# A hybrid decoder layer with sparse experts: scores moved into the first u piece, rows requested earlier, the sort's steps and transfers a piece apart, more v rows beside u blocks

## The chip, the cores and the metric

The kernel runs on one core of one Trainium2 chip. The metric is the device time of one execution in microseconds. The median of three runs of the kernel before is 3421.0 us (3416.03, 3421.0 and 3427.66).

## What is computed

One layer for 512 prompt tokens and 64 sample tokens (576 in all), width 2048: adaptive normalisation, one input projection, a gated linear recurrence and a short convolution, an output projection, and then PEER, a layer of 16384 single-neuron experts with product keys. The change touches PEER alone:

```python
def peer(h, w_q, sub_keys, expert_u, expert_v):
    ...
        q = (xb @ w_q).reshape(PEER_BLOCK, PEER_HEADS, 2, HALF_DIM)
        sc = jnp.einsum('thpk,pnk->thpn', q, sub_keys).astype(jnp.float32)
        v1, i1 = lax.top_k(sc[:, :, 0], PEER_TOPK)
        v2, i2 = lax.top_k(sc[:, :, 1], PEER_TOPK)
        cand = (v1[..., :, None] + v2[..., None, :]).reshape(...)
        cidx = (i1[..., :, None] * N_KEYS + i2[..., None, :]).reshape(...)
        top, pos = lax.top_k(cand, PEER_TOPK)
        eidx = jnp.take_along_axis(cidx, pos, axis=-1)
        g = jax.nn.softmax(top, axis=-1).astype(xb.dtype)
        act = jax.nn.gelu(jnp.einsum('td,thkd->thk', xb, expert_u[eidx])) * g
        return jnp.einsum('thk,thkd->td', act, expert_v[eidx])
```

Each token has 8 heads and 16 picks a head, 128 picks; a pick is a row of `expert_u` (2048 numbers) multiplied with the token, and a row of `expert_v` added to its result with a weight.

## The kernel before

**Dense blocks and gathered rows.** The first key of a pick names one of 128 blocks of 128 experts. For the prompt tokens the 84 blocks that are picked most (`L`) are computed densely on TensorE for all 512 tokens, with the gates of experts that were not picked at zero. What is left over of the prompt's picks, and all picks of the sample tokens, are gathered: an indirect transfer issued by POOL (`take`, L1131) brings one row for each of 128 partitions, a tile of 128 x 2048, and VectorE forms its product with the token (a u row, L1159, `u`) or adds it to a sum (a v row, L1185, `accB`). Tokens are put in groups for this (`GT`; group 0 is the samples, the others are prompt tokens sorted by the number of their left-over picks), so that a group of many picks gets many rows. There are 216 uses of u rows, in groups that end at uses 64, 99, 143, 177, 205 and 216, and 211 of v rows. Row buffers: 4 during the u phase (`RB`), 6 after it (`RV`). A use at a group's end reads the next group's token vectors first (`h2r`, L1140).

**Phases.** Until 1240.7 us of the span come the normalisation, the projections, the recurrence, the queries and their top 16. The u phase, 1240.7 to 2349.5, is 168 pieces, half a block each: 24 matmuls (L1270, `u_half`) on a 512 KB piece of the u table (`raw<-ut`, loaded by SP three pieces ahead) that ACT and POOL split two pieces ahead into a high and a low part (`xhi` L842, `xlo` L843). Each finished block goes through a Gelu and out to memory (`act`, `actd`). The v phase, 2349.5 to 3269, is 84 steps of four columns, 12 matmuls each (L1290, `v_column`), whose sums VectorE adds up (`acc`, L1312). The samples' sums and the final normalisation follow.

**What runs beside the u pieces.** The loop over the pieces `n` issues, ahead of the matmuls of each piece, some of the other work. An allowance `spare` grows by `PIECE` (5.5) a piece, beginning at `-BEHIND`; while it is positive, the next step of a generator is issued, and the cost that the step yields is taken off (also 2.4 for a used row and 2.2 for a pair of gate blocks). A `None` from the generator ends the piece's steps.

- `choice()` (`steps1`) comes first. It finishes the last head: scores of the sample tokens ("S") and of the four prompt tiles (`score`, matmuls and copies), `choose`, `resolve`, `softmax`. Then `count()` marks the picks outside the dense blocks (`flags`, L1000 to L1004) and writes the picked values to memory with eight transfers on POOL's queue (`pickd`, L1010 and L1011); twelve transposes (`ptr`, L1414) turn the picks for the gates (`it`, L1416); `sort()` ranks the tokens: `srt` (L1021), four steps z of comparing and one-hot building on VectorE (L1032, L1034, L1041) with five small matmuls each (ten passes in the trace; `tokp`, L1043), and a last sum (`overp`, L1058). When it ends, at piece `R1`, the gates begin.
- The gates, from `R1` on: 128 blocks of one-hot products, put together in pairs on VectorE (`g_pair`, L1449, `op` and `wr`), scaled on ACT (`g_scale`, L1457), multiplied on TensorE (`g_mm`, L1463, into `gbank`) and copied out by ACT (`g_out`, L1470). `g_one` issues a block's matmuls, once ahead of a piece and once in its middle (`mid`).
- `all_slots()` (`steps2`), also from `R1` on: for each group of tokens the rows it needs are picked out (`slot_rows`, `pick_keys`, L1066 to L1110). It ends at piece `R2`. `ready[0]` is the last use whose list is made.
- Rows: until `R2`, `gather_to` uses up `due_g`, which grows by the first number of `RATE` a piece before `R1` and by the second after it, and is held by `ready[0]`; a row is requested up to `RB - 1` uses ahead. After `R2` the remaining u rows and the first `EARLY_V` v rows are spread evenly over the pieces that are left.

In the built program of before, the lists of group 0 are ready at piece 6 and the first row is requested and used at piece 8; `R1` is 46 and `R2` is 147; 222 rows are used in the u phase.

Of the kernel before, what the change touches and what calls it, by code (L numbers as in the profile page):

```python
# [5 lines left out]
F32 = mybir.dt.float32  # L6
# [32 lines left out]
QT = NA // 128  # L39
SORTED = ((0, 64, 34), (64, 128, 43), (192, 128, 33), (320, 128, 27), (448, 64, 10))  # L40
RB = 4
# [1 line left out]
ENDS = 5  # L43
LATE = 1
PIECE = 5.5
BEHIND = 18.0
RATE = (0.75, 1.55)
HEADS_COUNTED = 4
FULL_ROWS = 1.25
LAG = 2  # L50
PAIRS = 6
EARLY_V = 6
HB = 4
SB = 10
TK = 16
# [21 lines left out]
def build(ctx, tc, A, O, dbg=None):  # L77
# [912 lines left out]
    def count():  # L990

        m = nd["m"] = rt.tile([128, 3, QT], F32, name="nd_m")
        fc = rq.tile([128, 2, NA], F32, name="flags", tag="oh", bufs=2)
        fl, code = fc[:, 0, :], fc[:, 1, :]
        i1, i2 = pbank("g", "i1", 2), iselP[:, 1, :]
        S.activation(i1, iselP[:, 0, :], AF.Copy)
        yield None
        V.tensor_scalar(fl, i1, perm[:, L:L + 1], None, op0=ALU.is_equal)
        for x in range(L + 1, 128):
            V.scalar_tensor_tensor(fl, i1, perm[:, x:x + 1], fl, op0=ALU.is_equal, op1=ALU.add)  # L1000
            if x % 8 == 7:
                yield 5.0
        V.scalar_tensor_tensor(code, i1, 128.0, i2, op0=ALU.mult, op1=ALU.add)
        V.scalar_tensor_tensor(code, code, 1.0, fl, op0=ALU.add, op1=ALU.mult)  # L1004
        V.tensor_reduce(m[:, 0, :], fl.rearrange("p (z k) -> p z k", k=NPK), axis=AX.X, op=ALU.add)
        for z in range(QT):
            V.tensor_scalar(m[:, 1, z:z + 1], rowi, float(128 * z), None, op0=ALU.add)
        V.scalar_tensor_tensor(m[:, 2, :], m[:, 0, :], float(NA), m[:, 1, :], op0=ALU.mult, op1=ALU.add)
        for z in range(QT):
            G.dma_start(pickd[z * 128:(z + 1) * 128, 0:NPK], code[:, z * NPK:(z + 1) * NPK])  # L1010
            G.dma_start(pickd[z * 128:(z + 1) * 128, NPK:], topv[z].rearrange("p h k -> p (h k)"))  # L1011
        yield 5.0
        for _ in range(2):
            yield None

    def sort():

        m = nd["m"]
        pr = pbank("g", "srt", 2)
        for z in range(QT):  # L1020
            PE.matmul(pr[:, z * 128:(z + 1) * 128], m[:, 2, z:z + 1].to_broadcast([128, 128]), ident, start=True, stop=True)  # L1021
        allk = pools["rsort"].tile([128, NA], F32, name="allk")
        S.activation(allk, pr, AF.Copy)
        io = pools["rsort"].tile([128, NA], F32, name="io512")
        for z in range(QT):
            V.tensor_scalar(io[:, z * 128:(z + 1) * 128], iota, float(128 * z), None, op0=ALU.add)
        yield None
        pt = pbank("g", "tokp", 2)
        rk = pools["rsort"].tile([128, QT], F32, name="rk")
        for z in range(QT):  # L1030
            oh = pools["rsort"].tile([128, NA], F32, name=f"ohs{z}", tag="ohs", bufs=2)
            V.scalar_tensor_tensor(oh, allk, m[:, 2, z:z + 1], ones[:, 0:1].to_broadcast([128, NA]),  # L1032
                                   op0=ALU.is_gt, op1=ALU.mult, accum_out=rk[:, z:z + 1])
            V.tensor_scalar(oh, io, rk[:, z:z + 1], None, op0=ALU.is_equal)  # L1034
            for i, (p0, n, c) in enumerate(GT):
                if p0 is None:
                    continue
                lhs = oh[:, p0:p0 + n]
                if n < 128:
                    lhs = pools["rsort"].tile([128, 128], F32, name=f"ohd{i}_{z}", tag="ohd", bufs=2)  # L1040
                    V.tensor_copy(lhs.rearrange("p (r t) -> p r t", t=n),  # L1041
                                  oh[:, None, p0:p0 + n].to_broadcast([128, 2, n]))
                PE.matmul(pt[:, 2 * i:2 * i + 2], lhs, m[:, 0:2, z], start=z == 0 and i == 1,  # L1043
                          stop=z == QT - 1 and i == len(GT) - 1)
            yield 4.0
        srt = pools["rsort"].tile([128, len(GT), 2], F32, name="sorted")
        V.memset(srt[:, 0, 0:1], 0.0)
        V.tensor_scalar(srt[:, 0, 1:2], rowi, float(NA), float(T - 1), op0=ALU.add, op1=ALU.min)
        V.tensor_copy(srt[:, 1:, :], pt[:, 2:2 * len(GT)].rearrange("p (i a) -> p i a", a=2))
        V.tensor_copy(tok, srt[:, :, 1])  # L1050

        for i, (p0, n, c) in enumerate(GT):
            cap = c * 128 // n if i else NPK
            V.tensor_scalar(srt[:, i, 0:1], srt[:, i, 0:1], -float(cap), 0.0, op0=ALU.add, op1=ALU.max)
        over = pools["rsort"].tile([128, 1], F32, name="over")
        V.tensor_reduce(over, srt[:, :, 0], axis=AX.X, op=ALU.add)
        pf = pbank("g", "overp", 2)
        PE.matmul(pf[:, 0:1], ones, over, start=True, stop=True)  # L1058
        V.tensor_copy(flag, pf[0:1, 0:1])
        yield 1.0  # L1060

# [152 lines left out]
    def gather_to(n, lim=1 << 30):  # L1214

        n = min(int(n), lim)
        while gu[0] < min(n, len(uses)):
# [4 lines left out]
            gu[0] += 1  # L1222
            flush(gu[0])

    def load_group(sg, j):

        if j == 0:
            acts[sg] = ep.tile([128, SG, NA], F32, name=f"actr{sg}", tag="actr", bufs=1)
            nc.scalar.dma_start(acts[sg], actd[SG * sg:SG * sg + SG].rearrange("i p t -> p i t"))
        else:  # L1230
            gsb[sg] = ep.tile([128, NCH, SG * TC], F32, name=f"gsb{sg}", tag="gsb", bufs=1)
            nc.scalar.dma_start(gsb[sg], gd[:, :, sg * SG:(sg + 1) * SG, :].rearrange("c p i t -> p c (i t)"))
# [20 lines left out]
    g2 = mods[5]  # L1253
    fin = {}

    def mid(n):
        if R1 is not None and gk:
            g_one(n)

# [111 lines left out]
    def choice():  # L1371

        side, h = {}, HD - 1
        order = ["S"] + late
        side["S"] = score(h, "S")
        picked = iter(())
        yield None
        for a, z in enumerate(order):
            if a + 1 < len(order):
                side[order[a + 1]] = score(h, order[a + 1])  # L1380
            choose(h, side[z], z)
            yield 6.0
            if z == "S":
                for _ in resolve("S", 0):
                    yield 9.0
                yield 5.0
                picked = pick_samples()
            yield next(picked, 0.0)
            yield next(picked, 0.0)
# [18 lines left out]
        for j in range(3):  # L1408
            it.append(itp.tile([128, NA], F32, name=f"it{j}"))
        for i in range(QT):  # L1410
            pt = pbank("g", f"ptr{i}", 2)
            t = topv[i].rearrange("p h k -> p (h k)")
            for j, src in enumerate((isel[i][:, 0, :], isel[i][:, 1, :], t)):
# [67 lines left out]

    E0 = NU2 - 14
    steps1, steps2 = choice(), all_slots()
    spare, due_g = -BEHIND, 0.0
    R1 = R2 = None
    gm = [0, 0, 0, 0]
# [12 lines left out]
    for n in range(NU2):  # L1499
# [3 lines left out]
        if n == 1:  # L1503
            sample_rows()
        ahead(n + 3, n + 2)
        spare += PIECE
        if R1 is not None:
            put(2)
            g_one(n)
# [9 lines left out]
            gm[3] = gm[0]  # L1519

        if R2 is None:
            due_g += RATE[R1 is not None] if ready[0] else 0
            g0 = gu[0]
            gather_to(due_g, ready[0])
            due_g = min(due_g, gu[0] + 1.0)
# [253 lines left out]
```

## Time and profile before

| | |
|---|---|
| median of three runs | 3421.0 us |
| profiled execution | 3418.08 us |
| its span | 3416.3 us |
| granted TensorE clock, mean | 0.961 |
| TensorE busy | 3196.4 us (94%) |
| VectorE, POOL, ACT busy | 2164.3, 1752.5, 1083.4 us |
| DMA | 868.17 MB, 254 GB/s in the mean |

Times in the profile are microseconds from the start of the span. TensorE is PE, VectorE DVE, ScalarE ACT, GpSimd POOL, SyncE SP. Each row of the groups has line, engine, operation, output and inputs, count, then busy time and the mean of one in ns, then the idle time ahead of it and what ended that. A row of waits names the waiting instruction's line, the one that ended the wait, the total, how many times, and the longest. A row of windows has the stretch and its length, the busy time and count of each engine asked for, the granted clock, the DMA engines' share and GB/s. Rows of the chain and of the timeline start with the time and the duration.

### The profile page before, as it was taken

What the parts mean: (1) busy time and instruction counts of PE and PEld (TensorE: products, weight loads), DVE (VectorE), ACT (ScalarE), POOL (GpSimd) and SP (SyncE); (2) the same over time, 40 slices, a digit from 0 to 9 for tenths busy, and PEclk for the clock granted to TensorE, in tenths of its full rate; (3) what the DMA queues carried; (4) which work ended last, traced back from release to release, by engine and by line L of the source; (5) the groups of instructions that cost most, each with busy time, mean ns of one, the idle gap of its engine ahead of it and who ended that gap; (6) DMA issues with size and microseconds to landing.
All of it is one profiled execution on the core that took longest, in us unless ns stands there. A gap on an engine that the chain in (4) does not pass through costs nothing.

```text
span 3416.3 us, 47510 instructions
## 1 busy us (share of the span) xinstructions
PE 3196.4 (94%) x17641; PEld 2710.3 (79%) x17641; DVE 2164.3 (63%) x3246; ACT 1083.4 (32%) x1665; POOL 1752.5 (51%) x993
## 2 busy tenths in 40 slices
PE   5899999989979999989999999998999999999887
PEld 2698788989969988878888888876888777777776
DVE  5355522143346887968786787766677777787735
ACT  3234311132232232315555555522322222222122
POOL 4233233344333336646555566566767766676742
PEclk8899999999989999989999999998999999999988
DMA  9644466634442137759986979899999988898954
GB/s 337 231 139 139 160 208 205 216 114 128 130 138 71 66 102 255 263 186 366 340 302 259 376 284 370 317 365 334 369 386 368 368 297 330 301 393 297 337 170 148
DMA packets 304029, 868.17 MB, mean 254 GB/s; under 512 B 36618, under 2 KB 80522, under 8 KB 255658
## 3 DMA queue, kind: packets, MB, share of 16 engines
q1 hardware_dynamic: 165152, 390.35, 33.5%
q0 software_dynamic: 62896, 386.64, 29.0%
q10 hardware_dynamic: 75744, 88.09, 7.3%
q8 instruction: 139, 2.28, 0.3%
q14 instruction: 98, 0.80, 0.1%
HBM read 864.69 MB, written 68.90 MB: 273 GB/s over the span
## 4 chain that ended last, share of the span: by engine, by line
PE 39%; DMA 9%; DVE 8%; issue 5%; POOL 3%; ACT 0%; SPq 0%; POOLq 0%; ACTq 0%; DVEq 0%
PE pu L1270 19%; PE pv L1290 15%; PE gbank L1463 3%; DMA v<-v,rows 3%; DMA gsb<-gd 2%; DMA actr<-actd 2%; DVE u L1159 2%; DVE accB L1185 2%; DMA raw<-v 1%; POOL xlo L843 1%; DVE flags L1000 1%; POOL u L1131 1%; DMA h2r<-h2d,tok 0%; DVE oh L728 0%; PE pv L1294 0%
## 5 line engine op out<-in xcount | busy, mean ns | idle before, releaser
L843 POOL TENSOR_TENSOR xlo<-raw,xhi 128x1024 fp32r<-128x1024 f32 x336 | 818.4, 2447 | 643.9 <-ACT xhi L842 637.0
L842 ACT ACTIVATE xhi<-raw 128x1024 fp32r<-128x1024 f32 x336 | 354.1, 1059 | 922.9 <-PE pv L1290 466.1
L1159 DVE SCALAR_TENSOR_TENSOR u<-u,hT 128x2048 f32<-128x2048 f32 x211 | 479.5, 2284 | 242.5 <-DMA u<-u,rows 242.0
L1185 DVE SCALAR_TENSOR_TENSOR accB<-v,dots,accB 128x2048 f32<-128x2048 f32 x205 | 482.4, 2353 | 156.3 <-DMA v<-v,rows 154.5
L1290 PE MATMUL pv<-ahi,xhi 128*128 128x512 f32 x1344 | 540.9, 402 | 31.3 <-DVE acc L1312 24.2
L1290 PE MATMUL pv<-ahi,xlo 128*128 128x512 f32 x1344 | 538.3, 401 | 17.0 <-POOL xlo L843 16.9
L1270 PE MATMUL pu<-hhi,xhi 128*128 128x512 f32 x1344 | 543.4, 404 | 4.3 <-ACT xhi L842 4.3
L1270 PE MATMUL pu<-hhi,xlo 128*128 128x512 f32 x1344 | 529.8, 394 | 7.5 <-POOL xlo L843 7.5
L1290 PE MATMUL pv<-alo,xhi 128*128 128x512 f32 x1344 | 534.8, 398 | 0.0
L1270 PE MATMUL pu<-hlo,xhi 128*128 128x512 f32 x1344 | 531.4, 395 | 0.0
L1290 PEld LDWEIGHTS pv<-ahi,xhi 128*128 128x128 f32 x1344 | 257.8, 192 | 93.1 <-issue 16.7
L1290 PEld LDWEIGHTS pv<-ahi,xlo 128*128 128x128 f32 x1344 | 257.3, 191 | 82.8 <-POOL xlo L843 22.8
L1270 PEld LDWEIGHTS pu<-hhi,xlo 128*128 128x128 f32 x1344 | 254.8, 190 | 67.8 <-POOL xlo L843 10.4
L1290 PEld LDWEIGHTS pv<-alo,xhi 128*128 128x128 f32 x1344 | 258.0, 192 | 58.6
L1270 PEld LDWEIGHTS pu<-hhi,xhi 128*128 128x128 f32 x1344 | 255.6, 190 | 57.5 <-ACT xhi L842 5.6
L1270 PEld LDWEIGHTS pu<-hlo,xhi 128*128 128x128 f32 x1344 | 255.5, 190 | 50.1
L1131 POOL DMA_INDIRECT v<-v,rows x211 | 249.2, 1181 | 58.3 <-issue 32.5
L1131 POOL DMA_INDIRECT u<-u,rows x211 | 221.3, 1049 | 72.1 <-DVE u L1159 32.3
L1457 ACT ACTIVATE op<-op,it 128x128 f32<-128x128 f32 x512 | 154.3, 389 | 0.0
L185 PE MATMUL ada<-wa,cpad 128*32 128x512 f32 x768 | 112.5, 691 | 42.9 <-DMA wa<-w_ada 42.9
L1463 PEld LDWEIGHTS gbank<-wr,op 128*128 128x128 f32 x1024 | 135.5, 193 | 18.7 <-ACT op L1457 8.0
L122 POOL TENSOR_TENSOR wlo_q<-raw_q,whi_q 128x1024 fp32r<-128x1024 f32 x28 | 67.4, 2407 | 146.1 <-ACT whi_q L120 146.1
(477 smaller groups left out, 5574.9 us busy)
## 6 DMA issues: line engine op xcount, KB each, us to landing
wa<-w_ada SPq DMA_DIRECT2D x96, 1024.0 KB, 6.4
raw<-ut SPq DMA_DIRECT2D x168, 512.0 KB, 5.8
raw<-v SPq DMA_DIRECT2D x336, 256.0 KB, 8.0
actd<-act ACTq DMA_DIRECT2D x84, 256.0 KB, 7.1
gd<-stg ACTq DMA_DIRECT2D x64, 336.0 KB, 8.8
actr<-actd ACTq DMA_DIRECT2D x21, 1024.0 KB, 21.3
gsb<-gd ACTq DMA_DIRECT2D x21, 1024.0 KB, 26.2
raw_o<-w_out SPq DMA_DIRECT2D x32, 512.0 KB, 3.8
```

What stands on the lines that cost most here:

```text
L122: lo_engine(share).tensor_sub(lo, raw, r32(hi))
L185: PE.matmul(acc[32 * g:32 * g + 32, :], cpad[:, 4 * kq + g, :], w[:, g, :], start=kq == 0, stop=kq == 3)
L842: S.activation(hi, raw, AF.Copy)
L843: G.tensor_sub(lo, raw, r32(hi))
L1000: V.scalar_tensor_tensor(fl, i1, perm[:, x:x + 1], fl, op0=ALU.is_equal, op1=ALU.add)
L1131: G.indirect_dma_start(out=out, out_offset=None, in_=src, in_offset=bass.IndirectOffsetOnAxis(ap=idx, axis=0), bounds_check=NE * 128 - 1, ...
L1159: V.scalar_tensor_tensor(r, r, 1.0, st["h"], op0=ALU.mult, op1=ALU.mult, accum_out=dots[i][:, j:j + 1])
L1185: V.scalar_tensor_tensor(st["a"], r, dots[i][:, j:j + 1], st["a"], op0=ALU.mult, op1=ALU.add)
L1270: PE.matmul(pu, st[:, kk, :], movA[mv](k), start=k == 0 and a == 0, stop=k == KD - 1 and a == 2)
L1290: PE.matmul(pv, st, mv, start=first and j == 0 and a == 0, stop=last and not end and j == SG - 1 and a == 2)
L1457: S.activation(ops[:, j0 + j, :], ops[:, j0 + j, :], AF.Copy, scale=it[2][:, b * 4 + j:b * 4 + j + 1])
L1463: PE.matmul(pg[:, j * L:(j + 1) * L], ops[:, j0 + j, :], wr[:, j0 + j, :], start=True, stop=True)
```

## The change

It has five parts.

1. The first step of `choice()` is issued in the middle of piece 0, and the scores of the samples and of the first prompt tile are both in it; before, it was issued where `spare` first allowed it, with the samples' scores alone. `BEHIND` falls from 18 to 7, so `spare` becomes positive earlier.
2. The piece after the lists of group 0 are ready is noted in `since`; two pieces before the first use three rows are requested together (`fetch_to`). Before, the first row was requested at the piece of its use.
3. `count()` ends its costed step, and one piece, ahead of the eight transfers on POOL's queue; the transposes are halved over two pieces; in `sort()` the matmuls of each z are issued behind the next z's VectorE work, with four buffers where there were two, and the end of the sort and its last sum stand a piece apart.
4. `RATE` rises from (0.75, 1.55) to (1.0, 1.7), and `spare` grows by 6.3 (`PIECE_G`) a piece from `R1` on, where it grew by 5.5.
5. `EARLY_V` rises from 6 to 20: 14 v rows more, all of group 0, are used in the u phase and as many fewer in the v phase.

In the built program after the change the group 0 lists are ready at piece 4, three rows are requested at piece 6 and the first is used at piece 8; `R1` is 53 and `R2` is 122; 236 rows are used in the u phase.

```diff
-BEHIND = 18.0
-RATE = (0.75, 1.55)
+BEHIND = 7.0
+RATE = (1.0, 1.7)
+PIECE_G = 6.3
...
-EARLY_V = 6
+EARLY_V = 20
...
+        yield 5.0
+        yield None
         for z in range(QT):
             G.dma_start(pickd[z * 128:(z + 1) * 128, 0:NPK], code[:, z * NPK:(z + 1) * NPK])
             G.dma_start(pickd[z * 128:(z + 1) * 128, NPK:], topv[z].rearrange("p h k -> p (h k)"))
-        yield 5.0
         for _ in range(2):
             yield None
...
+        hot = []
+
+        def count_up():
+            for out, lhs, rhs, first, last in hot:
+                PE.matmul(out, lhs, rhs, start=first, stop=last)
+            hot.clear()
+
         for z in range(QT):
...
+            todo_ = []
             for i, (p0, n, c) in enumerate(GT):
...
-                    lhs = pools["rsort"].tile([128, 128], F32, name=f"ohd{i}_{z}", tag="ohd", bufs=2)
+                    lhs = pools["rsort"].tile([128, 128], F32, name=f"ohd{i}_{z}", tag="ohd", bufs=4)
...
-                PE.matmul(pt[:, 2 * i:2 * i + 2], lhs, m[:, 0:2, z], start=z == 0 and i == 1,
-                          stop=z == QT - 1 and i == len(GT) - 1)
+                todo_.append((pt[:, 2 * i:2 * i + 2], lhs, m[:, 0:2, z], z == 0 and i == 1,
+                              z == QT - 1 and i == len(GT) - 1))
+            count_up()
+            hot.extend(todo_)
             yield 4.0
+        yield None
+        count_up()
...
         pf = pbank("g", "overp", 2)
+        yield None
         PE.matmul(pf[:, 0:1], ones, over, start=True, stop=True)
+        yield None
         V.tensor_copy(flag, pf[0:1, 0:1])
         yield 1.0
...
+    def fetch_to(n):
+        while gf[0] < n and row_free():
+            fetches[gf[0]]()
+            gf[0] += 1
...
+    mids = {}
+
     def mid(n):
+        for f in mids.pop(n, ()):
+            f()
         if R1 is not None and gk:
             g_one(n)
...
         order = ["S"] + late
-        side["S"] = score(h, "S")
+        for z in order[:2]:
+            side[z] = score(h, z)
         picked = iter(())
         yield None
         for a, z in enumerate(order):
-            if a + 1 < len(order):
+            if a and a + 1 < len(order):
                 side[order[a + 1]] = score(h, order[a + 1])
...
         for i in range(QT):
+            if i == 2:
+                yield None
             pt = pbank("g", f"ptr{i}", 2)
...
     steps1, steps2 = choice(), all_slots()
+    mids[0] = [lambda: next(steps1)]
+    since = None
...
-        spare += PIECE
+        spare += PIECE if R1 is None else PIECE_G
...
-            due_g += RATE[R1 is not None] if ready[0] else 0
+            if since is None and ready[0]:
+                since = n
+            if since is not None and n == since + 1:
+                fetch_to(RB - 1)
+            due_g += RATE[R1 is not None] if since is not None and n > since + 2 else 0
```

## The prediction

> **What bounds the kernel now.** I read the head of the page first, then cut the time from 1249.7 us on into stretches by counting TensorE's matmuls at the two lines that set the pace, and last read what PE waited for in the stretches that came out too long.
>
> ```profile
> span 3416.3 us, 47510 instructions
> PE 3196.4 (94%) x17641; PEld 2710.3 (79%) x17641; DVE 2164.3 (63%) x3246; ACT 1083.4 (32%) x1665; POOL 1752.5 (51%) x993
> ```
>
> PE is busy for 94% of the span. No matmul of the dense work is added or removed, so the change can only win or lose what PE loses. The stretches of the u phase (matmuls of L1270 only, 24 to a piece; columns: length, PE busy and matmuls, weight loads, granted clock, DMA share, GB/s) and of the v phase (L1290, 12 to a column):
>
> ```profile
> 1249.70:1472.80 223.10, 221.74 (x961) 179.95 (x962) 1.00 0.69 241
> 1472.80:1524.10 51.30, 26.40 (x98) 20.22 (x96) 0.77 0.42 154
> 1546.20:1692.50 146.30, 128.15 (x529) 96.98 (x528) 1.00 0.94 355
> 1692.50:1712.80 20.30, 13.97 (x49) 10.43 (x49) 0.83 0.95 367
> 1858.30:1877.80 19.50, 12.96 (x48) 9.66 (x48) 0.91 0.99 382
> 1877.80:2235.90 358.10, 314.62 (x1297) 238.65 (x1298) 1.00 0.89 339
> 2263.40:2349.50 86.10, 72.16 (x289) 55.54 (x288) 0.94 0.88 321
> ...
> 2349.50:2396.60 47.10, 38.95 (x144) 29.66 (x145) 0.86 0.97 356
> 2396.60:2663.20 266.60, 266.00 (x1154) 216.24 (x1153) 1.00 0.98 368
> 2663.20:3269.10 605.90, 568.50 (x2390) 456.53 (x2389) 0.97 0.89 325
> ```
>
> Undisturbed rates come from the rows with clock 1.00: 223.1 us for 961/24 = 40 pieces, 5.58 us each; 146.3 us for 22 pieces with gate blocks between them, 6.65 us; 266.6 us for 96 v columns, 2.78 us. The other rows are longer than their count at these rates. Four pieces (41 to 44) took 51.3 us, 29 over 4 x 5.58. Pieces 71/72 and 95/96 took 20.3 and 19.5, over 13.3: 7.0 and 6.2. The last 12 u pieces took 86.1, over 67: 19. The first 12 columns took 47.1, over 33.3: 14. The last v row took 605.9 us for 199 columns, over 553: 53. That is 128 us in six places; the waits of PE there say what was late.
>
> ```profile
> PE ptr L1414 <- ACT it L1416: 6.4, 1, 6.4
> PE tokp L1043 <- issue: 5.0, 1, 5.0
> PE ptr L1414 <- DVE flags L1003: 2.3, 1, 2.3
> ...
> PE gbank L1463 <- ACT op L1457: 3.3, 1, 3.3
> ...
> PE gbank L1463 <- ACT op L1457: 3.8, 1, 3.8
> ...
> PE pu L1270 <- POOL xlo L843: 7.5, 6, 1.7
> PE pv L1290 <- ACT acc L1310: 4.9, 1, 4.9
> ...
> PE pv L1290 <- DVE acc L1312: 24.2, 9, 5.7
> PE pv L1290 <- POOL xlo L843: 13.6, 6, 7.1
> ```
>
> In order: the sort (1472 to 1530), the two changes of row group (1686 to 1715, 1850 to 1880), the end of the u phase with the first columns (2235 to 2397), and the v phase after it. The idle time is smaller than the excess because PE is slow after a stall, seen at the first group change:
>
> ```profile
> 1703.94 0.63 PE L1270 MATMUL pu<-hlo,xhi 128*128 128x512 f32 x1
> ...
> 1711.07 0.39 PE L1270 MATMUL pu<-hhi,xlo 128*128 128x512 f32 x1
> ```
>
> The first kind takes 0.63 us, the second 0.39; some ten of the slow ones make 2.4 us, and I use 2.5 per stall. [...]
>
> **Part by part.** How pieces move I read from the order of the two built programs on each engine; only the prices are from the trace. Pieces are numbered from 0, and a step that the schedule puts "at" a piece is issued ahead of its matmuls.
>
> *The sort (before: pieces 41 to 44).* Its own matmuls stay, and its waits move:
>
> ```profile
> 1488.09 1.54 PE ptr L1414 x6
> 1496.73 0.89 PE srt L1021 x8
> 1508.07 8.66 PE tokp L1043 x40
> ...
> 1504.41 0.75 DVE L1032 SCALAR_TENSOR_TENSOR ohs<-allk,nd_m,ones 128x512 f32<-128x512 f32 x1
> ...
> 1508.02 0.74 DVE L1032 SCALAR_TENSOR_TENSOR ohs<-allk,nd_m,ones 128x512 f32<-128x512 f32 x1
> ```
>
> The flags end at piece 41, the picked values are written at 44, and the transposes come at 46 and 47. So the 6.4 and 2.3 us of waits go. The eight writes of picked values move with them on POOL's queue:
>
> ```profile
> L1010 POOL DMA_DIRECT2D pickd<-flags x4 | 2.2, 557 | 14.6 <-DVE flags L1004 14.6
> L1011 POOL DMA_DIRECT2D pickd<-topv x4 | 2.2, 548 | 0.0
> ```
>
> There they waited 14.6 us at the queue's head for the flags, with a row and a conversion behind them; issued three pieces after the flags they wait for nothing and hold the queue for 4.4 us, which the two-piece lead of the conversions hides (without it, 4.4 on PE). But by then the allowance has grown to 20, so all four 4.0 steps of the rank counting still run at one piece, 49: the spreading is only partly done. The matmuls of each z stand behind the next z's VectorE work, those of z 0 to 2 still ahead of piece 49, the last ones at 50. PE at 49 then waits for a row product and the first counts, about 7 us where it was 5.0 (the second product in line, 2.3, and one z, from 1504.41 to 1508.02 at most 3.6, mostly 1.9). Sum: transposes 2.4, srt 0.9, wait 7, z 0 to 2 6.5, slow restart 2.5, last z 2.2: 21.5 against 29, so -8. Bounds: -20 if the counts are ready in time, +2 if each z waits for its own row.
>
> *Slots of group 1.* In the old order its five steps fall at pieces 47 to 61; in the new one all five (5, 4, 4, 4, 4) fall at piece 54, and the first pair of gate blocks stands behind them on VectorE at 55.
>
> ```profile
> 1538.71 0.22 DVE L1066 TENSOR_SCALAR sl<-R 128x128 uint32<-128x128 uint32 x1
> ...
> 1544.24 0.28 DVE L1099 MATCH_REPLACE8 kk<-sl,kk 128x128 f32<-128x128 f32 x1
> 1544.44 1.21 DVE L1449 TENSOR_TENSOR op<-kb,it 128x1024 f32<-128x1024 f32 x1
> ...
> 1701.24 2.40 ACT L1457 ACTIVATE op<-op,it 128x128 f32<-128x128 f32 x8
> ```
>
> The first two steps took 5.7 us (1538.71 to 1544.44): 2.2 for the keys and 3.55 for each step of six picks, so 16.4 for all. With the row's product VectorE is about 5 us into piece 54 when it begins; then come the slots, the pair (2.1) and half the scaling (1.2): 24.7 us after piece 54 begins. The first gate matmuls are due before piece 57, 3 x 5.5 = 16.5 us after it. PE waits 8.2 and restarts slowly, 2.5: +10.7. Bounds: 0 if the slots are done under earlier row waits, +16.
>
> *Group changes.* Before, rows 64 and 99 on (groups 1 and 2) each waited for the next group's hidden rows, read only once the list was ready: 7.0 and 6.2. In the new order list 1 is ready at piece 64, where use 64 is reached, so the first stall stays. List 2 is ready when its use is far off (143 ready at piece 80, at 91 uses), so the second goes: -6.2. Bounds -13 and 0.
>
> *Scores inside piece 0 and earlier rows.* VectorE begins the last head three pieces earlier. PE has no wait in pieces 1 to 40 (221.74 of 223.10 us busy), so nothing is won there; what hides it is the same row of PE work. The rows of uses 0 to 2 are requested two pieces ahead, and VectorE's first wait for a row shrinks. Value 0, bounds -3 and +3 (scores' matmuls standing in front of piece 0's second half).
>
> *Rate and early v rows.* The new rates bring 64 uses by piece 64, where the old order had them at 68; the u phase ends with 236 rows used, where it was 222. Its last 16 pieces take 1.6 a piece and took 1.9, but the last 20 are full v rows.
>
> ```profile
> L1159 DVE SCALAR_TENSOR_TENSOR u<-u,hT 128x2048 f32<-128x2048 f32 x211 | 479.5, 2284 | 242.5 <-DMA u<-u,rows 242.0
> L1185 DVE SCALAR_TENSOR_TENSOR accB<-v,dots,accB 128x2048 f32<-128x2048 f32 x205 | 482.4, 2353 | 156.3 <-DMA v<-v,rows 154.5
> L1131 POOL DMA_INDIRECT v<-v,rows x211 | 249.2, 1181 | 58.3 <-issue 32.5
> ...
> q0 software_dynamic: 8249, 59.95, 56.6%
> ```
>
> At the u phase's end PE waits for xlo and xhi, made from raw blocks that came late. A row is 1 MB, a raw piece 0.5, the activations 0.13: 1.6 rows make about 2.2 MB in 5.58 us, 396 GB/s; 1.9 rows with fewer of them full made 2.15, 385. So little is relieved: -5 of the 19 (bounds +10 and -15). The v phase loses 14 rows of 205: 33 us of VectorE (14 x 2.35), 17 of POOL, and 14.7 MB of transfers, which at the 368 GB/s of its second row are 40 us of DMA time out of 919, or 4%. Its stalls come to 14 + 53 = 67 us, and most are accumulations queued behind products that wait for rows. I take a fifth of them, -14; bounds 0 (the columns run at full speed at share 0.98, so the stalls are not saturation alone) and -40 (all of that transfer time was late).
>
> [...]
>
> **Sum:** -8 + 10.7 - 6.2 + 0 - 5 - 14 = -22.5. The profiled execution took 3418.1 us, 1.8 beyond its span, and gives 3395.6. The median of the runs is 2.9 above the profiled time; between the two bases I say 3397.
>
> **Rivals.** *VectorE falls behind from piece 54 on (slower).* Between pieces 54 and 122 the new order puts 116 products, 45 pairs of gate blocks and the slots of four groups on VectorE: 116 x 2.21 (2.28 less the overlap with the next) + 45 x 2.07 + 65 (the slots of all groups, 103 planned units at the 5.7/9 of above) is 414 us, in 68 x 6.65 = 452 us of PE. That leaves 38 for waits. In 22 such pieces before, it waited for rows
>
> ```profile
> DVE u L1159 <- DMA u<-u,rows: 22.7, 17, 4.8
> ```
>
> so 68 pieces would ask for 70. If the rows stay as late as that, 32 us come out of PE through the gate blocks, with two more slow restarts: 3397 + 32 + 5 = 3434. Against it: a VectorE that is late finds its rows landed, and waits shrink. It decides once waits per piece stay above 38/68 = 0.56 us while PE waits for gate matmuls.
>
> [...]
>
> *The v phase's stalls go by most of their size*, -40, with the sort's waits hidden: 3397 - 26 - 6 = 3365. For it speaks that all three resources of a row are relieved at once; against it, that 14 rows in 205 leave 93% of the load.
>
> *The change doesn't spread the sort as it says*: this is in the forecast already, at pieces 49 and 54. If instead both lumps cost nothing, 3397 - 10.7 - 9.5 = 3377.
>
> **How the numbers follow.** Two measurements of this kernel tell apart about 0.3%, 10 us: faster is below 3411, slower above 3431. The forecast (3380 to 3410) has 0.45, the deep gain and the lumps at nothing 0.13, the lost v gain 0.16 (mostly within 0.3%), VectorE behind 0.26. Faster 0.45 + 0.13 = 0.58; slower 0.21 of VectorE's 0.26 and 0.03 of the lost gain's 0.16 = 0.24; the rest, 0.18, is the same. The range runs from 3366 to 3440: about a tenth lies below, in the deep gain, and a tenth above, beyond VectorE's price. The forecast's own range is 3378 to 3412.
>
> **What would show it.** Right: no PE wait at the transposes; one stall of 5 to 9 us at piece 49 and one at 57, each with slow matmuls behind it; one group stall instead of two; the last 12 u pieces in 80 us or so; v columns from 2663 on with less than 53 us over 2.78 each. Wrong: VectorE without row waits and PE waiting on ACT's scaling through pieces 57 to 122 (VectorE behind); unchanged DVE waits in the v phase (v rows free of charge); conversions late from piece 122 on (transfers).

## The result and the profile after

The changed kernel takes 3399.01 us (median of 8 runs, 3393.41 to 3406.68) beside 3423.73 us for the kernel before (8 runs, 3416.03 to 3433.95): ratio 0.9934, 95% interval 0.9917 to 0.9952. (The ratios here are those on record with their intervals; the two medians alone give 0.9928.) A second measurement gave 0.9940 (0.9918 to 0.9961). So the kernel is faster, by 0.6 to 0.7%, which is small but clear of the noise. The forecast was 3397, faster.

The head of the page of the changed kernel:

```profile
span 3396.0 us, 47497 instructions
PE 3183.6 (94%) x17641; PEld 2699.9 (80%) x17641; DVE 2155.1 (63%) x3246; ACT 1084.6 (32%) x1665; POOL 1739.4 (51%) x993
```

The span is 20.3 us shorter, 3.4 of it ahead of the u phase, which starts at 1237.3 instead of 1240.7. The change touches nothing there, and the start lay between 1237.3 and 1243.5 in the profiles of this study: 16.9 us remain. The windows of the u matmuls (now L1295) show where:

```profile
1237.30:1469.30 232.00, 226.79 (x984) 184.44 (x985) 1.00 0.78 269
1469.30:1510.10 40.80, 39.34 (x169) 31.23 (x168) 1.00 0.82 279
1510.10:1538.30 28.20, 13.23 (x48) 10.25 (x49) 0.76 0.55 218
1571.70:1597.00 25.30, 13.00 (x50) 9.71 (x48) 0.80 0.72 258
...
1651.00:1671.90 20.90, 13.88 (x49) 10.41 (x49) 0.84 0.92 350
1792.70:1809.60 16.90, 11.86 (x48) 8.77 (x49) 1.00 0.92 335
2057.70:2073.80 16.10, 11.83 (x49) 8.81 (x49) 1.00 1.01 411
...
2228.60:2345.90 117.30, 103.08 (x432) 82.56 (x432) 0.94 0.92 349
```

and those of the v matmuls (now L1315):

```profile
2345.90:2390.40 44.50, 38.40 (x145) 29.64 (x146) 0.84 0.94 346
2390.40:2664.30 273.90, 269.43 (x1153) 217.94 (x1152) 0.99 0.96 354
2664.30:3250.20 585.90, 559.95 (x2389) 451.35 (x2388) 0.98 0.86 315
```

Pieces 0 to 40 take 232.0, as before (9.0 + 223.1). Pieces 41 to 47 run freely (40.8 for seven, 1.7 over their rate), where four pieces lost 29 before. The sort's stall is now at 48/49 (28.2 for two, 17.0 over), a new one is at 56/57 (25.3, 14.1 over, some 2 of it gate blocks), the first group change is at 66/67 (7.6 over 13.3), the second at 86/87 (3.6 over), and a small one has come at 125/126 (2.8 over). So pieces 0 to 150 lost 2.6 us net. From 150 to the first column it is 117.3 where it was 120.1, the first 12 columns take 44.5 (47.1 before), the next 96 are slower at 273.9 (266.6), and the 199 after them take 585.9 (605.9). That is 307 of the 336 columns; the other 29 come after 3250 (after 3269 before), among the last work on the samples. PE's waits between 1490 and 2236, from there to 2397, and from there to 3269:

```profile
PE gbank L1491 <- ACT op L1485: 13.3, 2, 9.3
PE tokp L1036 <- issue: 7.7, 1, 7.7
PE gbank L1491 <- ACT stg L1498: 4.7, 2, 2.7
...
PE pv L1315 <- ACT xhi L843: 9.2, 1, 9.2
PE pv L1315 <- POOL xlo L844: 6.1, 3, 3.2
...
PE pv L1315 <- POOL xlo L844: 17.1, 5, 7.8
PE pv L1315 <- DVE acc L1337: 13.3, 9, 3.0
```

The two waits at the transposes are gone. PE waits 7.7 us for the counting (7 in the forecast) and 9.3 for the first gate operands (8.2 in the forecast), and the accumulations that held the v columns for 24.2 us now hold them for 13.3. VectorE's timeline at piece 48 tells why PE waits for the counting: two more products and the index rows (`io`) stand ahead of the first z.

```profile
1514.74 2.29 DVE L1175 SCALAR_TENSOR_TENSOR u<-u,hT 128x2048 f32<-128x2048 f32 x1 [1.84 <-DMA u<-u,rows]
1516.95 0.08 DVE L1175 DVE_READ_ACCUMULATOR u<-u,hT 128x1 f32 x1
1516.95 2.76 DVE L1028 TENSOR_SCALAR io<-iota 128x128 f32<-128x128 f32 x4
1519.68 2.29 DVE L1175 SCALAR_TENSOR_TENSOR u<-u,hT 128x2048 f32<-128x2048 f32 x1
...
1521.89 0.75 DVE L1041 SCALAR_TENSOR_TENSOR ohs<-allk,nd_m,ones 128x512 f32<-128x512 f32 x1
```

### The profile page after: what moved, and what is told of

Its sections match the earlier page's. It is cut to its first block, busy times and chain, and to the rows that moved or that the text cites. A ratio compares the mean times of both kernels' runs of the same rounds, so it can differ in the third digit from the quotient of the medians.

```text
span 3396.0 us, 47497 instructions
## 1 busy us (share of the span) xinstructions
PE 3183.6 (94%) x17641; PEld 2699.9 (80%) x17641; DVE 2155.1 (63%) x3246; ACT 1084.6 (32%) x1665; POOL 1739.4 (51%) x993
## 4 chain that ended last, share of the span: by engine, by line
PE 51%; DMA 4%; issue 4%; DVE 2%; POOL 2%; ACT 0%; POOLq 0%; SPq 0%; ACTq 0%; DVEq 0%
PE pu L1295 24%; PE pv L1315 23%; PE gbank L1491 3%; DMA v<-v,rows 2%; POOL xlo L844 1%; DMA u<-u,rows 1%; POOL v L1147 1%; PE pv L1319 0%; DMA tok<-accd 0%; DMA raw<-v 0%; DVE kk L1115 0%; DVE acc L1677 0%; DMA h2r<-h2d,tok 0%; PE tokp L1036 0%; PE ph L1378 0%
## 5 line engine op out<-in xcount | busy, mean ns | idle before, releaser
L1315 PE MATMUL pv<-ahi,xhi 128*128 128x512 f32 x1344 | 538.4, 401 | 22.6 <-DVE acc L1337 13.3
L1315 PE MATMUL pv<-ahi,xlo 128*128 128x512 f32 x1344 | 535.8, 399 | 23.2 <-POOL xlo L844 23.2
L1295 PE MATMUL pu<-hhi,xhi 128*128 128x512 f32 x1344 | 541.9, 403 | 2.2 <-ACT xhi L843 2.2
L1315 PE MATMUL pv<-alo,xhi 128*128 128x512 f32 x1344 | 532.5, 396 | 0.0
L1295 PE MATMUL pu<-hhi,xlo 128*128 128x512 f32 x1344 | 529.0, 394 | 2.2 <-POOL xlo L844 2.2
L1295 PE MATMUL pu<-hlo,xhi 128*128 128x512 f32 x1344 | 530.6, 395 | 0.0
L1315 PEld LDWEIGHTS pv<-ahi,xlo 128*128 128x128 f32 x1344 | 256.0, 191 | 87.2 <-POOL xlo L844 27.6
L1315 PEld LDWEIGHTS pv<-ahi,xhi 128*128 128x128 f32 x1344 | 256.3, 191 | 84.3 <-ACT xhi L843 15.4
L1315 PEld LDWEIGHTS pv<-alo,xhi 128*128 128x128 f32 x1344 | 256.4, 191 | 58.0
L1295 PEld LDWEIGHTS pu<-hhi,xlo 128*128 128x128 f32 x1344 | 254.1, 189 | 60.3 <-POOL xlo L844 3.1
L1295 PEld LDWEIGHTS pu<-hhi,xhi 128*128 128x128 f32 x1344 | 255.2, 190 | 54.8 <-ACT xhi L843 2.6
L1295 PEld LDWEIGHTS pu<-hlo,xhi 128*128 128x128 f32 x1344 | 254.8, 190 | 50.1
L1147 POOL DMA_INDIRECT v<-v,rows x211 | 240.9, 1142 | 60.2 <-issue 38.0
L1491 PEld LDWEIGHTS gbank<-wr,op 128*128 128x128 f32 x1024 | 135.5, 194 | 30.6 <-ACT op L1485 14.1
L1491 PE MATMUL gbank<-wr,op 128*128 128x84 f32 x1024 | 132.7, 273 | 18.0 <-ACT op L1485 13.3
```

Of the source, the lines that this page charges most:

```text
L1147: G.indirect_dma_start(out=out, out_offset=None, in_=src, in_offset=bass.IndirectOffsetOnAxis(ap=idx, axis=0), bounds_check=NE * 128 - 1, ...
L1295: PE.matmul(pu, st[:, kk, :], movA[mv](k), start=k == 0 and a == 0, stop=k == KD - 1 and a == 2)
L1315: PE.matmul(pv, st, mv, start=first and j == 0 and a == 0, stop=last and not end and j == SG - 1 and a == 2)
L1491: PE.matmul(pg[:, j * L:(j + 1) * L], ops[:, j0 + j, :], wr[:, j0 + j, :], start=True, stop=True)
```

## The experiments

Each kernel was run in five rounds beside the kernel before, on four chips in all; so the ratios are compared and not the times. The stages below (us) are worked out from each trace: first matmul of piece 0, of piece 150, of the first and of the last v column. "Used" is the number of rows that the built program has used by piece 150.

| kernel | early v rows | used | 0 to 150 | 150 to v | v | ratio to before (95%) |
|---|---|---|---|---|---|---|
| before | 6 | 190 | 988.7 | 120.1 | 1036.5 | 1 |
| changed | 20 | 209 | 991.3 | 117.3 | 1019.8 | 0.9934 (0.9917 to 0.9952) |
| changed, again (e5) | 20 | 209 | 992.2 | 114.7 | 1016.8 | 0.9940 (0.9918 to 0.9961) |
| e1 six v rows | 6 | 200 | 989.5 | 101.5 | 1045.8 | 0.9965 (0.9948 to 0.9981) |
| e8 v rows alone | 20 | 193 | 984.1 | 164.1 | 1026.5 | 1.0087 (1.0064 to 1.0109) |
| e9 old rates | 20 | 198 | 993.6 | 146.9 | 1024.9 | 1.0056 (1.0037 to 1.0076) |
| e4 old sort | 20 | 208 | 988.6 | 116.5 | 1022.6 | 0.9944 (0.9924 to 0.9965) |
| e2 slots apart | 20 | 207 | 977.8 | 120.6 | 1022.2 | 0.9941 (0.9921 to 0.9962) |
| e3 z apart too | 20 | 205 | 970.3 | 123.8 | 1025.5 | 0.9935 (0.9912 to 0.9957) |
| e7 gates later | 20 | 207 | 991.9 | 117.1 | 1014.8 | 0.9945 (0.9925 to 0.9964) |
| e6 split later | 20 | 209 | 991.4 | 110.2 | 1016.2 | 0.9937 (0.9914 to 0.9959) |
| e11 z apart, split later | 20 | 206 | 980.4 | 117.5 | 1018.7 | 0.9936 (0.9915 to 0.9957) |
| e10 the same, rates up | 20 | 210 | 993.9 | 107.9 | 1019.7 | 0.9949 (0.9930 to 0.9968) |
| e12 vectors on VectorE | 20 | 205 | 961.7 | 112.0 | 1028.9 | 0.9871 (0.9849 to 0.9893) |

**Which part carries the gain.** e1 takes the v rows back out, e4 the new sort, e9 the rates; e8 puts the v rows alone into the kernel before.

```diff
e1, e8 (the other way round, in the kernel before):
-EARLY_V = 20
+EARLY_V = 6
e9:
-RATE = (1.0, 1.7)
-PIECE_G = 6.3
+RATE = (0.75, 1.55)
+PIECE_G = 5.5
e4: count(), the transposes and sort() as before the change
```

> The changed kernel with the number of early v rows put back from 20 to 6; all else as changed, the sort and the slots at the same pieces. Changed kernel: 3399 us. The forecast's account (14 v rows less are worth 14 us in the v phase, and the end of the u phase pays some us for them): the v phase 10 to 16 us longer, the last 12 u pieces up to 6 shorter, the whole 3405 to 3412. Rival (the v phase's gain has another source, such as another alignment of rows and columns, or the rows cost beside u blocks what they save later): 3393 to 3402, the v columns from 2397 us on no longer than in the changed kernel.

> The changed kernel with the counting, the transposes and the sort as before the change (transfers and transposes in one piece, each z's matmuls behind its own VectorE work); scores in piece 0, rows ahead, rates and 20 v rows stay. The sort then ends earlier, the gates begin at piece 49, and the allowance is used up, so the slots of group 1 fall at 50, 54, 57, 60 and 63. Account: the sort's pieces cost 29 us over their rate and not 17 (+12), and the wait at piece 56 for the first gate operands goes (-12): 3395 to 3403, so that the third part of the change is worth nothing by itself. Rival (the wait for the gates comes from the rates and stays): 3408 to 3414.

> The kernel before with 20 early v rows and nothing else changed. The 14 rows more all fall at pieces 148 to 167, where 53 rows are then used, 2.6 a piece: about 3.2 MB in 5.5 us, which is more than the 420 GB/s that the busiest slices show. Account (rows left in the v phase are worth about 1 us each and more, but only where transfers have room beside the u pieces): the last 20 u pieces 15 to 25 us longer, the v phase 12 to 25 shorter, the whole 3412 to 3425, no change. Rival (the v rows moved are the whole of the change's gain, and the early start only makes the sort's and the slots' trade): 3398 to 3407.

> The changed kernel with the two rates and the allowance per piece as before the change (0.75, 1.55, 5.5); 20 early v rows, the new sort and the early start stay. 198 rows are used by piece 150 (changed kernel 209, kernel before 190), so 38 fall on the last 17 pieces, 2.2 a piece. Account (the gain of the v rows is had only if the rates have cleared u rows out of the last pieces first): from piece 150 to the first column 130 to 145 us, between the 117 of the changed kernel at 1.6 a piece and the 164 of the v rows alone at 2.6, the v phase 1015 to 1026, and the whole 0.998 to 1.006 of the kernel before. Rival (the early start and the sort carry the gain): 0.990 to 0.995.

e1: as the account expected in the sum, with larger terms: the v phase is 26 us longer than in the changed kernel, and the stretch ahead of it 16 shorter. e4: as the account expected; the third part of the change is worth nothing by itself here. The old sort ends earlier and leaves no heap of allowance, and PE has no wait for scaled gate operands in e4, but two for gate copies, 10.1 us together. e8: outside both expectations, slower by 0.9%: 44 us are lost from piece 150 to the first column and 10 won in the v phase. e9 is slower too, by 0.6%, as its account expected (the stretch ahead of the v phase, 146.9, is just above the 130 to 145 of it).

So the early v rows can't be had without the rates: the rates clear u rows out of the last pieces, and only then do 14 v rows fit. The other way round it works: e1 has the rates (with the new sort and the early start) without the v rows, and is faster than the kernel before by 0.35%, clear of the noise. From piece 150 to the last column it takes 1147.3 us, where the kernel before takes 1156.6 and the changed kernel 1137.1 and 1131.5 in its two profiles. By these profiles the rates are worth 9 us there and the 14 v rows 10 to 16 on top of them; in the ratios the v rows' share is 0.3%, at the edge of what the intervals tell apart.

What breaks in e8? The expectation said that the rows are more than the transfers can carry. In its stretch from piece 150 to the first column the DMA engines have a mean share of 0.87 (the last but one number):

```profile
2224.60:2388.70 164.10, 115.06 (x432) 87.87 (x432) 0.87 0.87 336
```

The waits of POOL in the same stretch of e8:

```profile
POOL u L1131 <- DVE u L1159: 26.6, 16, 4.2
POOL v L1131 <- DVE dots L1181: 14.5, 1, 14.5
POOL v L1131 <- DVE accB L1185: 8.7, 7, 2.4
```

and those of PE:

```profile
PE pu L1270 <- POOL xlo L843: 25.7, 13, 5.2
PE pv L1290 <- ACT xhi L842: 12.2, 1, 12.2
PE pu L1270 <- ACT xhi L842: 10.5, 1, 10.5
```

A row is requested by POOL into one of four buffers. When none is free, the request waits at the head of POOL's queue until VectorE has used the oldest row (for u rows 16 times in this stretch of e8, 26.6 us in all), and the conversion `xlo` of the next piece stands behind it. Of POOL's waits the 14.5 us are another case: VectorE's `dots` stood behind its weighting `actr`, which itself waited 11.3 us for activations. The changed kernel's POOL, from piece 150 to the first column:

```profile
POOL v L1147 <- DVE accB L1201: 6.9, 4, 2.3
```

It waits 7 us where e8 waits 52 (2.3 of it in a line not shown); in e1 no such wait is over 0.2 us. But the kernel before waits 28 us there, and its stretch is only 3 us longer than the changed kernel's:

```profile
POOL u L1131 <- DVE u L1159: 23.8, 12, 4.4
...
POOL v L1131 <- DVE u L1159: 4.2, 2, 2.3
```

So the waits of POOL don't give the time by themselves, and neither does the record rule out the transfers:

| kernel | rows used in the stretch | POOL's requests wait for VectorE (us) | GB/s | MB (GB/s x length) | length (us) |
|---|---|---|---|---|---|
| e1 | 22 | 0.2 | 305 | 31.0 | 101.5 |
| changed | 27 | 7 | 349 | 40.9 | 117.3 |
| before | 32 | 28 | 348 | 41.8 | 120.1 |
| e9 | 38 | 37 | 338 | 49.7 | 146.9 |
| e8 | 43 | 52 | 336 | 55.1 | 164.1 |

In the last four the DMA engines move 336 to 349 GB/s, nearly the same, so the bytes at that rate give the length about as well as the rows do. A mean share of 0.87 isn't room either: cut into stretches of 15 us, e8's has shares of 1.01 to 1.03 in five of eleven and 0.57 to 0.84 in the others. In its first 38 us ACT also waits 14.1 us for raw pieces of the u table.

With 20 early v rows the stretch from piece 150 to the last column goes by the rows used until then: 193 give 1190.6 us, 198 give 1171.8, 205 (e3) 1149.3, and 209 give 1137.1 and 1131.5 in two profiles. That is 3.5 us a row ((1190.6 - 1134.3) / 16), with a scatter: e7 with 207 has 1131.9. A fifth buffer during the u phase was not tried, so it stays open whether the buffers, the requests or the bytes set the limit.

**The two lumps.** e2 cuts the allowance to 0 when the gates begin, e3 spreads the counting besides, and e7 keeps the allowance but starts the gates' pieces later.

```diff
e2, e3:
                 if R1 is None:
                     R1 = n
+                    spare = min(spare, 0.0)
e3, e7:
             hot.extend(todo_)
             yield 4.0
+            yield None
e7:
-        return min(NB2, max(0, (n - R1) * NB2 // (E0 - 6 - R1)))
+        return min(NB2, max(0, (n - R1 - 3) * NB2 // (E0 - 9 - R1)))
```

> The changed kernel, but the allowance is cut to 0 when the gates begin (piece 53), so that the slots of group 1 fall at pieces 54, 58, 60, 64, 65 and 66 and not at 54 alone; list 1 is then ready at piece 67 where it was 64. Account: the 9.3 us wait of PE for the first scaled gate operand and the slow restart behind it go, some 12 us, the group stall at use 64 stays (8): 3385 to 3390. Rival (VectorE is loaded either way, and what it no longer does at 54 makes it late at 58 to 66, or the later list makes the group stall longer): 3395 to 3402, with PE waits for ACT's scaling summing to 13 us or more between pieces 54 and 70.

> As the run with the allowance cut to 0, and besides one z of the rank counting a piece (pieces 49 to 52) where all four fell at 49; the gates begin at piece 57. Account: the 7.7 us wait at the counting's matmuls and its slow restart go as well, since each z has a piece's time: 3375 to 3382, and the matmuls themselves (9 us) stay. Rival (each z waits behind its own row product, so that PE waits four times for a shorter while, or the four pieces that the gates begin later make their rate a bound): no better than the run before it, 3385 to 3395.

> The changed kernel, one z of the rank counting a piece, the allowance not cut, so the slots of groups 1 and 2 all fall at piece 58, and the gates' pieces begin three later (61): 207 rows are used by piece 150, as in the run with z apart (205) and the changed kernel (209). Account (what a stall loses before piece 150 is won if it goes, and from piece 150 on the time goes by the rows that are left, about 1 us each: 237 left 1157 us, 228 left 1147, 218 left 1137): no PE wait at the counting, none for the first gate operands, no group stall, u pieces to 150 25 to 32 us shorter, from 150 on 1 to 5 longer: 20 to 30 us below the changed kernel. Rival (the end of the u phase and the v phase are bound by transfers as a whole, so that an earlier arrival there is mostly given back, as two thirds of 24 us were with z and slots apart): 5 to 12 us below.

PE's waits between 1460 and 2236 in e2:

```profile
PE tokp L1036 <- issue: 7.6, 1, 7.6
PE gbank L1491 <- ACT stg L1498: 3.4, 2, 3.2
PE gbank L1491 <- ACT op L1485: 2.9, 1, 2.9
```

and in e3:

```profile
PE gbank L1492 <- ACT op L1486: 3.7, 1, 3.7
PE gbank L1492 <- ACT stg L1499: 2.7, 3, 1.1
PE tokp L1036 <- ACT xhi L843: 2.3, 1, 2.3
```

The 9.3 us wait goes with the lump and the counting's 7.6 with z apart, and pieces 0 to 150 get 14 and 22 us shorter than in e5 (the changed kernel again), as the account said. But the whole gets no faster than the changed kernel within the interval, so both totals miss the account (3395.3 us each, where 3385 to 3390 and 3375 to 3382 were expected): in e3 the stretch behind piece 150 is 18 us longer than in e5 (1149.3 against 1131.5), with four rows fewer used by then. e7 won nothing, outside both of its expectations, because seven slot steps (32 units) then ran at piece 58 and the gates, three pieces later, waited 13 us for them.

**A late copy at the head of a queue.** Ahead of the first v column ACT waits for VectorE, with the conversions for that column behind it (ACT's waits of the changed kernel, 2330 to 2347):

```profile
ACT ahi L1265 <- DVE actr L1258: 17.5, 1, 17.5
```

e6 moves this weighting and split two pieces later, e10 and e11 combine it with z apart (allowance cut to 8), e10 with higher rates.

```diff
e6, e10, e11, e12:
-            if n - E0 == o + 4 - sg:
+            if n - E0 == o + 4 + sg:
...
+    halve(1, 1)
e10, e11 (0.0 in e12):
+                    spare = min(spare, 8.0)
e10:
+RATE = (1.0, 1.85)
+PIECE_G = 6.65
```

> The changed kernel itself, as the base on this chip for the other three: 0.992 to 0.995 of the kernel before. By pieces: about 17 us shorter from the start of the u phase to the last column, most of it (10 to 18 us) between the first v column and the last; the start of the u phase itself, 1237 to 1244 us in six profiles, is no part of the change.

> The changed kernel; the weighting and splitting of the second group of activations stand two pieces later (166 to 168 instead of 164 to 166), so that on ACT's queue the split (ahi) comes behind the conversions of the first two v pieces. Account (a queue's order: the transfer of activations is late under more rows, VectorE waits for it, ACT waits 17.5 us for VectorE at the head of its queue, and the first v conversions stand behind): the 9.2 us wait of PE at the first v column goes down to 2 or less, and the run is 6 to 10 us below the changed kernel on the same chip. Rival (the transfers as a whole are late, and the wait only moves into the next columns): within 3 us of it.

> The changed kernel with one z of the counting a piece, the allowance cut to 8 when the gates begin (three slot steps at piece 58), the rate after that 1.85 instead of 1.7 and the allowance per piece 6.65 instead of 6.3, and the split of the second group of activations two pieces later; 210 rows are used by piece 150, as in the changed kernel (209). Account (a stall's gain before piece 150 is kept if no more rows are left then): pieces 0 to 150 in 968 to 975 us (changed kernel 992), from 150 on 1125 to 1135 (changed kernel 1131 to 1137), the whole 0.985 to 0.989 of the kernel before. Rival (VectorE has no room for the higher rate, so that PE waits for the gate operands again): pieces 0 to 150 in 980 or more, the whole 0.991 to 0.995.

> As the run with z apart and the higher rate, but with the rates of the changed kernel (1.7 and 6.3): 206 rows are used by piece 150, and 30 fall on the last 17 pieces. Account: pieces 0 to 150 in 968 to 975 us as well, from 150 on 3 to 10 us longer than with the higher rate (1130 to 1143), the whole 0.988 to 0.992 of the kernel before. Rival (the rows left at piece 150 have no part in what is given back): the same from 150 on as with the higher rate, within 2 us.

e5 lands on the first measurement. In e6 the wait at the first column went from 6.3 us (e5) to 1.0 and its profile is 6 us shorter than e5's, but the runs (0.9937 against 0.9940) can't tell that from nothing: the account had the wait right, the rival the time. e10 is a miss, and the numbers of its rival came: pieces 0 to 150 lose all of their gain, and most of PE's waits there are not at the slots (the 5.1 us) but for the copy of the gates out of PSUM:

```profile
PE gbank L1492 <- ACT stg L1499: 18.4, 6, 6.9
PE gbank L1492 <- ACT op L1486: 5.1, 1, 5.1
```

e11 has the same two kinds (9.5 and 5.1 us) and misses too, with 980.4 us to piece 150 (968 to 975 expected) and 0.9936; from there on it is 9 us longer than e10, as its account said. In e10, at the longest of these (6.9 us, piece 87), ACT's longest wait, from 1770 to 1825, is

```profile
ACT hT L1163 <- DMA h2r<-h2d,tok: 9.9, 1, 9.9
```

the copy of the next group's token vectors into PSUM, at the head of ACT's queue; gate copies and scalings stand behind it. e12 gives that copy to VectorE, in the kernel of e3 with the later split.

```diff
-            S.activation(st["h"], r, AF.Copy)
+            V.tensor_copy(st["h"], r)
```

> The run with z and slots apart (allowance cut to 0, gates from 57 on), with the split of the second group of activations two pieces later, and with one more edit: the copy of the next group's token vectors into PSUM (L1162, hT), which waits 8 to 10 us at the head of ACT's queue at a group change for the vectors' transfer, is made by VectorE. Account (the gate stalls that are left, PE on ACT's op and stg copies at the group changes, are a queue's order: ACT waits at its head, its conversions, scalings and gate copies stand behind, and they have less lead than VectorE's pairs): pieces 71/72 of that run 7.5 us shorter, pieces 0 to 150 in 955 to 965 us (970 with the copy on ACT), from 150 on 1138 to 1148, the whole 0.986 to 0.990 of the kernel before. Rival (VectorE, which then waits at its own head and works 2.2 us more a group, hands its pairs on late, and the stall stays at the same place): pieces 0 to 150 in 968 to 976, the whole 0.991 to 0.994.

PE's waits between 1460 and 2236 in e12:

```profile
PE tokp L1036 <- ACT xhi L843: 2.3, 1, 2.3
PE gbank L1492 <- ACT stg L1499: 1.1, 1, 1.1
```

and VectorE's group of the copies, from 1240 to 2350:

```profile
L1163 DVE COPY hT<-h2r 128x2048 f32<-128x2048 f32 x5 | 11.5, 2295 | 22.2 <-DMA h2r<-h2d,tok 22.1
```

VectorE now waits 22 us for the vectors and works 11.5 us more, and PE loses almost nothing: 961.7 us to piece 150, inside the account's 955 to 965. The split moved later acts from piece 164 on, so up to piece 150 e3 and e12 differ by the copy alone, and that is worth 8.6 us (970.3 to 961.7; three profiles with the changed kernel's first 150 pieces, those of the changed kernel, e5 and e6, agree within 1 us). Behind piece 150 the copy and the split can't be told apart, since no run has e3 with the later split alone; e11, the nearest, cuts the allowance to 8. With 0.9871 (0.9849 to 0.9893), 3378.57 us beside 3423.46, e12 beats both kernels.

## Why the prediction was right, and where it was off

**The time and the direction** came out as forecast: -22.5 was the sum, and the medians differ by 24.7 and in the second measurement by 20.9. By stages, from the first u piece to the last column, the profiles have -16.9 and -21.6 (e5). Part of the agreement is luck: in the first profile the terms below are off by up to 4 us each, in both directions.

**From piece 150 on** the forecast was -5 - 14 = -19, and the two profiles of the changed kernel have -19.5 and -25.1 (1137.1 and 1131.5 against 1156.6). The accumulations' waits fell from 24.2 to 13.3 as expected. Right in size, but for a reason only partly right. I priced rates and early v rows as one, while e1, e8 and e9 show that the rows cost 34 us without the rates (1190.6 against 1156.6) and gain with them. I read PE's waits for `xlo` as raw blocks that came late, and overlooked that POOL in the kernel before waited 28 us in that stretch for row buffers, with conversions behind. And the -14 was a fifth of the stalls, a share that no row gave. Of the signs named for being wrong one is there: VectorE's waits for v rows (before, then changed, 2397 to 3269) hardly changed.

```profile
DVE accB L1185 <- DMA v<-v,rows: 143.7, 71, 12.7
...
DVE accB L1201 <- DMA v<-v,rows: 140.3, 53, 14.6
```

So the v rows were not free of charge (e1, where PE's waits for accumulations are 28.5 us), but VectorE does not wait less for those that are left; the size of the term was right, and how the 14 rows bring it is open. The +10 that was the upper bound for the end of the u phase is in neither profile of the changed kernel: from piece 150 to the first column it takes 2.8 us less than the kernel before, and 5.4 less in e5. Nor did the case come that had 0.16 of the chances, a v phase that wins nothing: it took 1019.8 and 1016.8 us after 1036.5. Whether e8's loss of 44 us came from the transfers or from POOL's queue, no run decides.

**The sort** was put at -8 and measured -10.3 (29 before; 1.7 + 17.0 after). The wait was right (7.7 for 7), and transposes and `srt` cost less than counted, since pieces 41 to 47 hardly notice them. The 2.5 for a slow restart came from durations that overlap: in the timeline of the first group change in the kernel before, matmuls start 0.43 us apart while slow (1703.94, 1704.37) and 0.23 apart later (1710.84, 1711.07), so ten slow ones cost 2.0.

**The lump at piece 54** was put at +10.7 and measured +12 (14.1 less two gate blocks); e2 takes it out, and its 9.3 us wait is gone.

**The group changes** are the step that failed. I had the first stay (7.0; measured 7.6) and the second go (6.2 to 0), because the list would be ready long ahead. The list was ready, but 3.6 us stayed at 86/87, so the two together brought -2.0 in place of -6.2. ACT's waits around 86 show what was late:

```profile
ACT hT L1162 <- DVE u L1175: 5.6, 1, 5.6
```

The copy into the one PSUM tile waited 5.6 us at ACT's head for VectorE's last product of the old group, though the list was ready. So the wait that I had read as one for a list was here one for a place in a queue; in e12, with the copy off ACT, no wait of PE at a group change is over 1.1 us.

The 2.8 us at 125/126 are no group change (the token vectors are copied at pieces 66, 86, 111, 131 and 149). There ACT waits for a pair of gate blocks that stands on VectorE behind products whose rows came up to 2.3 us late:

```profile
ACT op L1485 <- DVE op L1477: 4.6, 1, 4.6
```

**Scores in piece 0** were put at 0 and are 0: piece 0 is 1.3 us longer and the forty after it 1.4 shorter.

**VectorE falling behind** did not come in the changed kernel up to piece 122; the 2.8 us at 125/126 are all that shows of it. Its waits for rows between 1560 and 2037.5 were

```profile
DVE u L1175 <- DMA u<-u,rows: 64.7, 40, 7.0
```

near the 70 that the rival asked for, or 0.95 a piece, above its threshold of 0.56; yet PE's gate waits stayed at the places named. The rival counted its 68 pieces at 6.65 us, 452; the window was 477 us with the lump in it, and VectorE was busy for 404, so that about all the time was used and PE lost nothing to it elsewhere. With the rate a tenth higher (e10) PE's gate waits grew, at the copies behind `hT`.

**Not settled:** why what e2 and e3 win before piece 150 is lost behind it beyond the 3.5 us a row. e3 lost 18 us for four rows, 14 by that price, and single profiles of one kernel differ by 6 there (e5 against the first).

## What to carry to other kernels

Price a transfer that is moved in the stretch that it is moved into, by the queue that requests it and its buffers as well as by bytes: with 20 early v rows each row that was left over at piece 150 went with 3.5 us here, and nothing separated the two causes. An edit that loses alone (the v rows 0.9%, or 0.6% with the new sort and early start but without the rates) can win on top of another, so undo the parts one at a time before judging any. When an engine that feeds the busy one waits at its queue's head for a slow copy, try giving the copy to an engine whose consumers have more lead: that one line took 8.6 us of the u phase, and together with the two lumps spread and the split moved 0.6 to 0.7%, as much again as the whole change.

## What was not expected of the hardware

The start of the u phase moved by 6 us (1237.3 to 1243.5) between profiles of kernels that are alike up to there, so stages have to be compared from their own start. VectorE's copy of 128 x 2048 values into PSUM took 2.30 us (e12) where ACT's took 1.88 (e3), and the slower engine was the better place.
